# Token columns loaded at the start, earlier adding transfers, new strand shares: a six-stage hybrid network on one core

## The chip, the core and the metric

The kernel runs on one core of a Trainium2 chip. The metric is the device time of one execution in microseconds (us). TensorE appears as PE (its weight loads as PEld), VectorE as DVE, ScalarE as ACT, GpSimd as POOL, and SyncE as SP, which issues most of the transfers.

## What is computed

A two-layer network on 256 tokens of width 1024, in fp32: six stages, each followed by a residual sum and a layer norm. Four stages are gated feed-forward networks (FFN, width 2816), one is a hybrid of a gated delta rule and a state-space scan (SSD), one is a sparse attention (NSA).

```python
def swiglu(x, w_in, w_out):
    gate, up = jnp.split(x @ w_in, 2, axis=-1)
    return (jax.nn.silu(gate) * up) @ w_out
...
h = x
for layer in range(DEPTH):                 # DEPTH = 2
    h = layer_norm(ALPHA * h + 0.5 * swiglu(h, ffn_w_in[layer, 0], ffn_w_out[layer, 0]), ...)
    mix = hybrid_mixer(h, ...) if layer % 2 == 0 else nsa_mixer(h, positions, ...)
    h = layer_norm(ALPHA * h + mix, ...)
    h = layer_norm(ALPHA * h + 0.5 * swiglu(h, ffn_w_in[layer, 1], ffn_w_out[layer, 1]), ...)
```

The hybrid stage projects `h` to queries, keys, values and gates of the delta rule and of the scan, runs both over the tokens in chunks, and projects the two results back. The sparse attention adds three attentions (over compressed blocks, over chosen blocks, over a window) under gates, and projects back.

## The kernel before

**Stages.** FFN1 runs to about 172 us, the hybrid to 420, FFN2 to 583, FFN3 to 757, the NSA stage to 895, FFN4 to the end.

**Products.** Each large product is made of three with operands of a shorter format: high x high, low x high, high x low. SP loads a weight tile as it is (512 KB, `raw`), ACT writes its high part (`whi`, `split` at L660), DVE subtracts for the low part (`wlo`). The token columns have the same two parts (`x`, high and low, tokens as columns by blocks of 128 features) and, in an FFN, the whole values (`X`), from which `token_forms` (L734) makes sums for a product scheme with seven products in place of eight (`wide`, L751; parts `fhi`, `flo`).

**An FFN** (`ffn`, L1044) goes over its 2816 hidden columns in 22 blocks of 128 (`f`). Blocks 0 to 3 come first (in FFN1 by `first_steps`, L1011: two passes over the input, gate columns, then up columns, 48 products each, and in the other FFNs by row tiles). Blocks 4 and 5 come by column tiles. The rest come in `CHUNKS` = 4 chunks of four blocks by `wide`. Between the seven products of a chunk, `flush` does terms of the second matrix: for a block `f`, `out_mm` multiplies the block's activation (`gh`, `gl`) with row tile `f` of `w_out` into the four banks of `acc`. `weights_to` loads row tiles three ahead (`AHEAD`).

**Adding transfers.** For the row tiles of `ADDED` (8, 10, ..., 20: seven in an FFN, 28 in all) DVE does not make the low part: ACT writes minus the high part into `wlo`, and a transfer from POOL's queue adds the weight from memory to it (`rows`, L705). Tiles live in slots of one pool; `W` (raw, high and low parts) may use 28 of them, with 14 kept for it.

**The head.** `run` (L2103) starts with products on constants (`spin`), then loads the tokens row by row into `h0`, `h1` in four transfers of 256 KB (`load`), in between the first weight tiles (`first_weights`, L717, with `arrivals`), and transposes them on PE in sixteen 128 x 128 products (`transpose_half`); ACT and DVE copy the results out as `x` and `X`. `h0`, `h1` stay as the residual.

**The order.** A planner (`Plan`, L187) lists all operations first, prices each (L269), and then sets one order for each engine (`order`, L352), by when an operation's inputs are ready and a priority. All instructions come out at L561 (`emit`), so the trace has that line throughout. Inside the hybrid and the NSA stage the strands are interleaved by `weave` (L885) in proportion to shares: `W_HYB` for (delta, space, gate, space2, out_a), `W_NSA` for (attention, dense, compressed, out_g0). `dense` (L1875) are projections that wait for nothing but weights, `out_g0` (L2089) the first products of the output projection.

Of the kernel before, what the change touches and what calls it, by code (L numbers as in the profile page):

```python
# [50 lines left out]
CHUNKS, AHEAD, LAG = 4, 3, 7  # L51

TERMS = ((0, 1, 1, 1, 1, 1, 1), (0, 0, 1, 1, 1, 1, 0), (0, 0, 1, 1, 1, 1, 0), (0, 0, 1, 1, 1, 0, 0))

ADDED = range(8, 22, 2)

STRANDS = ("mp",)
W_HYB, W_NSA = (60.0, 140.0, 25.0, 40.0, 15.0), (70.0, 60.0, 40.0, 20.0)
# [3 lines left out]
RANK = 0  # L62

# [118 lines left out]
class Op:  # L182
    __slots__ = ("eng", "fn", "args", "kw", "idx", "prio", "cost", "table", "deps", "succ", "ndep", "ready", "start",
                 "end", "alloc", "dense", "alts", "tiles", "nbytes", "quad", "port", "banks")


class Plan:  # L187
# [11 lines left out]
    def __init__(self):  # L199
        self.ops = []  # L200
        self.tiles = []
        self.base = 0
        self.gate = None
        for e in ("tensor", "vector", "scalar", "gpsimd", "sync"):
            setattr(self, e, _Eng(self, e))
# [7 lines left out]
    def add(self, eng, fn, args, kw, alts=None):  # L213
# [3 lines left out]
        op.alts = alts  # L217
        op.deps, op.succ, op.alloc, op.nbytes = {}, [], None, 0
# [133 lines left out]
    def order(self, caps):  # L352
# [27 lines left out]
        port = 0.0  # L380
# [67 lines left out]
        while left:  # L448
            best = None
            for e in engs:  # L450
# [6 lines left out]
                for op in lst:  # L457
# [16 lines left out]
                    key = (st if st > f + 1e-9 else f, p)  # L474
                    if cand is None or key < cand[0]:
                        cand = (key, op, pen)
# [5 lines left out]
            (key, op, pen), e = best  # L482
            st = key[0] + pen
# [23 lines left out]
            if fn == "dma_start":  # L507

                at, need = st + 1300, op.nbytes * (2 if e == "gpsimd" else 1)
                while need > 0:  # L510
                    n = int(at / 500)
                    room = (155e3 if at < 8000.0 else 190e3) - moved.get(n, 0)
                    take = min(need, room, room * (n + 1 - at / 500), 95e3 if e == "gpsimd" else need)
# [3 lines left out]
                op.end = at + 600  # L517
# [67 lines left out]
class K:  # L585
    NT = 2
# [130 lines left out]
    def first_weights(self, w, n0, arrivals):  # L717

        out = []
        for n in range(4):  # L720
            src = w[n0 + n]
            raw = self.m4(1024, "raw", "W")
            hi, lo = (self.m4(1024, name, "W", F32R) for name in ("whi", "wlo"))
            step = 512 if arrivals and n < 2 else 1024
            for e in range(0, 1024, step):
                cs = slice(e, e + step)
                self.nc.sync.dma_start(raw[:, cs], src[:, cs])
                self.split(hi[:, cs], lo[:, cs], raw[:, cs])
                for f in (arrivals.pop(0) if arrivals else []):
                    f()  # L730
            out += [(hi[:, k * 512:k * 512 + 512], lo[:, k * 512:k * 512 + 512]) for k in range(2)]
        return out
# [207 lines left out]
    def layer_norm(self, b, acc, s, gb, x, last):  # L940
# [70 lines left out]
    def first_steps(self, x, w_in, gtiles, gts):  # L1011
# [4 lines left out]
        for c0, tag, arrivals in ((0, "acc", self.arrivals), (DFF, "ps", [])):  # L1016
# [15 lines left out]
        for b in range(2):  # L1032
# [6 lines left out]
            for f in range(4):  # L1039
                self.split(gts[f][0][:, b * P:(b + 1) * P], gts[f][1][:, b * P:(b + 1) * P], pt[:, f * P:(f + 1) * P])  # L1040
            with _Gate(self.plan, len(self.plan.ops) - 1):
                self.scale_h(b)

    def ffn(self, l, j, x, then, last=False):  # L1044
# [5 lines left out]
        NT = self.NT  # L1050
# [10 lines left out]
        def out_mm(b, f, g, wo, cols=range(2)):  # L1061
            for c in cols:
                cs = slice(c * 512, (c + 1) * 512)
                bs = slice(b * P, (b + 1) * P)
                n = count[b, c] = count.get((b, c), 0) + 1
                self.mm3(acc[b][c], (g[0][:, bs], g[1][:, bs]), (wo[0][:, cs], wo[1][:, cs]), n == 1,
                         n == NF - (ENDS if last and b == 1 and c == 1 else 0))
# [4 lines left out]
        else:  # L1072
# [4 lines left out]
            for b in range(2):  # L1077
                for s in range(NT):
                    ps = self.bank("ps")
# [12 lines left out]
        terms, late, wos = [], [], []  # L1092
# [1146 lines left out]
```

## Time and profile before

| | |
|---|---|
| three runs | 1090.65, 1086.72, 1089.8 us, median 1089.8 us |
| the profiled execution | 1087.19 us, its span (first to last instruction) 1085.5 us |
| mean granted TensorE clock | 0.995 of full speed |
| busy: PE, DVE, ACT | 1066.3, 1010.9, 725.9 us of the span |

The span leaves 1.7 us of the execution's time outside. Engines work side by side, so a busy time says only how long an engine had work; what its waits cost is to be seen at each place. The clock of a stretch is either its full level (2.4 GHz, 1.00) or its half (1.2 GHz, 0.50), or a mean of the two.

### The profile page before, as it was taken

The numbers are of one execution on the slowest core, as the hardware profiler recorded it, in microseconds if no ns is written. First come the engines' busy times: TensorE is split into PE (matmuls) and PEld (weight loads), VectorE is DVE, ScalarE is ACT, GpSimd is POOL, SyncE is SP. The second block draws the span as 40 slices with busy tenths as digits, with TensorE's granted clock in tenths as the row PEclk, the third lists the DMA queues.
The fourth block names the chain that finished last, engine by engine and source line by source line (L and its number), as shares of the span: only waits on it lengthen the run. The fifth ranks groups of instructions, "written<-read, shape, count | busy, mean of one in ns | idle before, by whom it ended". The sixth has DMA issues, their size and how long they took to land.

```text
span 1085.5 us, 16212 instructions
## 1 busy us (share of the span) xinstructions
PE 1066.3 (98%) x5946; PEld 893.3 (82%) x5946; DVE 1010.9 (93%) x1453; ACT 725.9 (67%) x1155; POOL 70.7 (7%) x116
## 2 busy tenths in 40 slices
PE   8999999998999999999999999999999999999997
PEld 6788888897999788888888888888887778888886
DVE  7999999799979999999999999999978889999995
ACT  7767866368737774667866667678465778666780
POOL 1000000001001310000000000000001000000000
PEclk9999999999999999999999999999999899999999
DMA  8658768535433575367777736679563336457881
GB/s 330 231 196 256 221 233 284 179 135 182 140 115 99 194 269 180 117 230 251 215 229 254 257 125 215 235 241 303 189 214 98 92 123 216 152 188 236 255 231 41
DMA packets 65034, 215.71 MB, mean 199 GB/s; under 512 B 8301, under 2 KB 12218, under 8 KB 64954
## 3 DMA queue, kind: packets, MB, share of 16 engines
q1 hardware_dynamic: 60922, 199.98, 52.8%
q0 software_dynamic: 4032, 14.68, 7.2%
q8 instruction: 47, 0.77, 0.3%
q14 instruction: 33, 0.27, 0.1%
HBM read 211.86 MB, written 1.07 MB: 196 GB/s over the span
## 4 chain that ended last, share of the span: by engine, by line
PE 84%; DVE 12%; ACT 1%; DMA 1%; issue 1%; POOL 0%; SPq 0%; DVEq 0%; ACTq 0%
PE ps L561 39%; PE acc L561 31%; PE mp L561 14%; DVE wlo L561 2%; DVE cv L561 2%; DVE arena L561 1%; DMA raw<-in_ffn_w_in_dram 1%; DVE o L561 1%; DVE sw L561 1%; DVE x L561 1%; DVE y L561 1%; DVE qs L561 1%; DVE AT L561 0%; POOL arena L561 0%; DVE Y L561 0%
## 5 line engine op out<-in xcount | busy, mean ns | idle before, releaser
L561 ACT ACTIVATE whi<-raw 128x1024 fp32r<-128x1024 f32 (+1 forms) x435 | 436.8, 1052 | 104.0 <-DVE raw L561 85.4
L561 DVE TENSOR_TENSOR wlo<-raw,whi 128x1024 fp32r<-128x1024 f32 (+2 forms) x419 | 491.4, 1205 | 7.1 <-ACT whi L561 6.1
L561 PE MATMUL ps<-whi,x 128*128 128x512 f32 (+1 forms) x864 | 234.8, 390 | 0.3 <-ACT cv L561 0.3
L561 PEld LDWEIGHTS ps<-whi,x 128*128 128x128 f32 x864 | 156.7, 188 | 30.6 <-issue 1.5
L561 DVE TENSOR_TENSOR raw<-raw,raw 128x1024 f32<-128x1024 f32 x128 | 152.8, 1216 | 0.0
L561 PE MATMUL ps<-wlo,x 128*128 128x512 f32 (+1 forms) x432 | 127.1, 385 | 0.0
L561 PE MATMUL ps<-x,whi 128*128 128x256 f32 (+2 forms) x560 | 114.3, 312 | 4.0 <-ACT cv L561 2.4
L561 PEld LDWEIGHTS ps<-x,whi 128*128 128x128 f32 (+1 forms) x560 | 90.4, 188 | 11.4 <-ACT cv L561 3.8
L561 PE MATMUL acc<-whi,gh 128*128 128x512 f32 x253 | 99.3, 393 | 0.0
L561 PE MATMUL acc<-wlo,gh 128*128 128x512 f32 x253 | 99.0, 391 | 0.0
L561 PE MATMUL acc<-whi,gl 128*128 128x512 f32 x253 | 97.9, 390 | 0.0
L561 PEld LDWEIGHTS ps<-wlo,x 128*128 128x128 f32 x432 | 79.6, 188 | 15.3 <-issue 0.4
L561 PE MATMUL ps<-x,wlo 128*128 128x256 f32 (+1 forms) x344 | 80.0, 284 | 0.5 <-DVE wlo L561 0.5
L561 PE MATMUL acc<-whi,x 128*128 128x512 f32 x224 | 73.7, 405 | 2.3 <-DVE x L561 0.8
L561 PE MATMUL acc<-whi,g 128*128 128x512 f32 x192 | 63.3, 392 | 0.0
L561 POOL DMA_DIRECT2D wlo<-in_ffn_w_out_dram x28 | 24.4, 872 | 569.2 <-ACT wlo L561 391.3
L561 PEld LDWEIGHTS ps<-x,wlo 128*128 128x128 f32 (+1 forms) x344 | 58.1, 189 | 2.1 <-DVE wlo L561 0.7
L561 PEld LDWEIGHTS acc<-whi,gl 128*128 128x128 f32 x253 | 47.5, 188 | 9.8
L561 PEld LDWEIGHTS acc<-whi,gh 128*128 128x128 f32 x253 | 47.5, 188 | 9.5
L561 PEld LDWEIGHTS acc<-wlo,gh 128*128 128x128 f32 x253 | 47.5, 188 | 9.5
L561 PEld LDWEIGHTS acc<-whi,x 128*128 128x128 f32 x224 | 41.8, 189 | 11.8 <-ACT whi L561 2.1
L561 PE MATMUL mp<-whi,fhi 128*128 128x512 f32 x128 | 49.9, 390 | 0.0
(284 smaller groups left out, 1735.2 us busy)
## 6 DMA issues: line engine op xcount, KB each, us to landing
raw<-in_ffn_w_in_dram SPq DMA_DIRECT2D x174, 512.0 KB, 5.5
raw<-in_ffn_w_out_dram SPq DMA_DIRECT2D x88, 512.0 KB, 3.7
wlo<-in_ffn_w_out_dram POOLq DMA_DIRECT2D x28, 512.0 KB, 8.5
raw<-in_hyb_w_col_dram SPq DMA_DIRECT2D x28, 512.0 KB, 4.5
raw<-in_hyb_w_tok_dram SPq DMA_DIRECT2D x16, 512.0 KB, 7.8
raw<-in_hyb_w_out_dram SPq DMA_DIRECT2D x16, 512.0 KB, 3.7
raw<-in_nsa_w_tok_dram SPq DMA_DIRECT2D x8, 512.0 KB, 6.6
raw<-in_nsa_w_one_dram SPq DMA_DIRECT2D x8, 512.0 KB, 5.8
```

The lines of the kernel that those rows point to most:

```text
L561: r = getattr(getattr(nc, eng), fn)(*[res(a) for a in args], **{k: res(a) for k, a in kw.items()})
```

## The change

1. **Tokens as columns.** The host hands the tokens over a second time, in the layout of the columns (`x_cols`). Four transfers of 256 KB bring them straight into `X`, each ahead of one of the first weight tiles (`first_loads`). ACT and DVE make `x` from `X` in four operations each of 512 columns. The transposes, the copies out of them, and the arrivals are gone. `h0`, `h1` are loaded later, in two transfers of 512 KB, for the residual alone. Of the first weight tiles only the first comes in halves. The spins are two of 512 columns.
2. **Adding transfers.** An added row tile is loaded two tiles earlier than the others (`EARLY`), and its low-part products are made one term later (`OWED`, `pay`). The planner prices the adding transfers anew (`ADD_RATE`, `ADD_LATE`, one after the other).
3. **Shares.** `W_HYB` and `W_NSA` have new numbers.
4. **A head start** of 135 ns, in the planner's choice, for the layer norm's operations on DVE and ACT (`HOT`).
5. **The rates' exponential** in the hybrid now waits in the plan for the sigmoid's exponential (`_Gate`).

`CHUNKS` becomes a tuple with 4 in all places, so the code for five chunks isn't used.

```diff
-ADDED = range(8, 22, 2)
+ADDED, EARLY, OWED = range(8, 22, 2), 2, 1
-W_HYB, W_NSA = (60.0, 140.0, 25.0, 40.0, 15.0), (70.0, 60.0, 40.0, 20.0)
+W_HYB, W_NSA = (51.0, 98.0, 22.0, 45.0, 20.0), (100.0, 67.0, 63.0, 21.0)
+HOT = 135.0
+ADD_RATE, ADD_LATE = 130e3, 4000.0
...
-                    key = (st if st > f + 1e-9 else f, p)
+                    at = st - HOT if op.hot and e in ("vector", "scalar") else st
+                    key = (at if at > f + 1e-9 else f, p)
...
+    def first_loads(self, x, w):
+        raws = []
+        for n in range(8):
+            if n < 4:
+                nc.sync.dma_start(x[1][n // 2][:, :, n % 2 * 2:n % 2 * 2 + 2, :],
+                                  self.i['x_cols'][n].rearrange("p (b k t) -> p b k t", b=2, k=2))
+            raw = self.m4(1024, "raw", "W")
+            for cs in [slice(0, 512), slice(512, 1024)] if n == 0 else [slice(0, 1024)]:
+                nc.sync.dma_start(raw[:, cs], w[n][:, cs])
+            raws.append(raw)
...
-            w = self.first_weights(w_in, 4 if c0 else 0, arrivals)
+            for n in range(4):
+                if c0 == 0:
+                    hi, lo = (x[0][n][:, :, e] for e in range(2))
+                    self.split(hi, lo, x[1][n // 2][...])
+                w += self.first_weights(raws.pop(0), [slice(0, 1024)] if c0 or n else [slice(0, 512), slice(512, 1024)])
...
+            with self.late():
+                nc.sync.dma_start(self.ah[b], self.i['x'][0, b * P:(b + 1) * P])
...
-            while len(wos) < min(n, NF):
-                wos.append(self.rows(w_out, len(wos), len(wos) in ADDED))
+            for f in range(NF):
+                if f not in wos and f < n + EARLY * (f in ADDED):
+                    wos[f] = self.rows(w_out, f, f in ADDED)
...
+                hi = (0,) if f in ADDED else (0, 1)
+                for b in both:
+                    out_mm(b, f, g, wos[f], parts=hi)
+                if f in ADDED:
+                    owed.append((done, both, f, g))
+                pay(done - OWED)
...
-        nc.scalar.activation(rate, rate, AF.Exp)
         self.sigmoid(beta, sm[:, :, 0:8])
+        with _Gate(self.plan, len(self.plan.ops) - 3):
+            nc.scalar.activation(rate, rate, AF.Exp)
...
-        spin(4, 2)
+        spin(4, 4)
...
-        load(0, 0)
-        with _Gate(self.plan, len(self.plan.ops) - 3):
-            spin(2, 2)
-        self.arrivals = [[], [lambda: load(1, 0)], [], [lambda: load(0, 1), lambda: load(1, 1)]]
```

**What moves at the head, on PE.** `ones` are the spins, `mp<-ident,h` the transposes, `acc<-whi,x` the first pass. Before:

```order
L561 MATMUL acc_124<-ones_109 128x512
L561 MATMUL acc_124<-ones_109 128x256
L561 MATMUL mp_143<-ident_126,h_3_111 128x128 x4
L561 MATMUL acc_161<-whi_151,x_157 128x512 x4
L561 MATMUL acc_124<-ones_109 128x256
L561 MATMUL acc_161<-wlo_167,x_157 128x512
L561 MATMUL acc_124<-ones_109 128x256
L561 MATMUL acc_161<-wlo_167,x_157 128x512
L561 MATMUL mp_178<-ident_126,h_5_116 128x128 x4
L561 MATMUL mp_183<-ident_126,h_3_111 128x128 x4
```

Now:

```order
L573 MATMUL acc_128<-ones_109 128x512 x2
L573 MATMUL acc_168<-whi_163,x_157 128x512 x2
L573 MATMUL acc_172<-whi_163,x_157 128x512 x2
L573 MATMUL acc_168<-whi_163,x_157 128x512 x2
L573 MATMUL acc_172<-whi_163,x_157 128x512 x2
L573 MATMUL acc_168<-wlo_166,x_157 128x512 x2
L573 MATMUL acc_172<-wlo_166,x_157 128x512 x2
L573 MATMUL acc_168<-whi_187,x_177 128x512 x4
```

Only the two spins stand ahead of the first pass, and nothing stands between its products. On ACT the scaling of the residual (`h`) now stands ahead of the high part of the first column tile (`whi_318`, blocks 4 and 5); it stood behind all four of these and two more. Now on ACT:

```order
L573 ACTIVATE whi_264<-raw_140 128x1024
L573 ACTIVATE sg_275<-acc_172 128x512
L573 ACTIVATE fhi_284<-X_3_111 128x1024
L573 ACTIVATE fhi_296<-X_8_123 128x1024
L573 ACTIVATE h_43_262<-h_43_262 128x512 x2
L573 ACTIVATE h_45_266<-h_45_266 128x512 x2
L573 ACTIVATE whi_318<-raw_268 128x1024
```

`whi_318` thus waits for the transfers of `h_43` and `h_45`, which stand ahead of its own on SP's queue too.

**What moves with an added tile, on PE.** `gh`, `gl` are the activation's parts of block 8 of FFN1, the first added one. Before, low-part and high-part products stand together:

```order
L561 MATMUL acc_605<-whi_912,gh_850 128x512
L561 MATMUL acc_605<-wlo_903,gh_850 128x512
L561 MATMUL acc_605<-whi_912,gl_859 128x512
L561 MATMUL acc_613<-whi_912,gh_850 128x512
L561 MATMUL acc_613<-wlo_903,gh_850 128x512
```

Now the high-part products come first, and some forty rows of the list later the four of the low part:

```order
L573 MATMUL acc_528<-whi_709,gh_803 128x512
L573 MATMUL acc_528<-whi_709,gl_812 128x512
L573 MATMUL acc_537<-whi_709,gh_803 128x512
L573 MATMUL acc_537<-whi_709,gl_812 128x512
...
L573 MATMUL acc_528<-wlo_701,gh_803 128x512
L573 MATMUL acc_537<-wlo_701,gh_803 128x512
L573 MATMUL acc_543<-wlo_701,gh_803 128x512
L573 MATMUL acc_555<-wlo_701,gh_803 128x512
```

No product is added; four of one term are made a term later.

**What moves at the end of the attention, on PE.** `ps<-whi,x` and `ps<-wlo,x` are the dense strand, `ident` and `kd`, `qs` the attention, `acc<-whi,x` the output projection. Before, the last dense product and what follows:

```order
L561 MATMUL ps_8350<-whi_8196,x_7693 128x512
L561 MATMUL ps_8506<-fixed_3924 128x512
L561 MATMUL mp_8509<-ident_126,P_8352 128x128 x2
L561 MATMUL mp_8509<-ident_126,P_8395 128x128 x2
...
L561 MATMUL mp_8573<-ident_126,arena_8273 128x128
L561 MATMUL mp_8577<-arena_7865,qT_1476_7874 128x32 x4
L561 MATMUL mp_8594<-ident_126,P_8430 128x128 x2
...
L561 MATMUL acc_8626<-whi_8215,x_8472 128x512
```

Now:

```order
L573 MATMUL ps_8304<-whi_8161,x_7658 128x512
L573 MATMUL mp_8509<-ident_132,P_8426 128x128
L573 MATMUL mp_8513<-ident_132,P_8426 128x128
...
L573 MATMUL ps_8521<-fixed_4059 128x512
L573 MATMUL acc_8543<-whi_8183,x_8356 128x512
L573 MATMUL acc_8543<-wlo_8191,x_8356 128x512
L573 MATMUL acc_8543<-whi_8183,x_8356 128x512
L573 MATMUL mp_8555<-ident_132,P_8426 128x128 x2
```

Between the last dense product and the first of the output projection stood 31 rows of the list; now there are 12, and from there on projection and attention alternate.

## Rows read from the trace of the kernel before

**Rows 1.** The page's first part: busy time of each engine, its share of the span and its instructions, of the whole execution.

```profile
PE 1066.3 (98%) x5946; PEld 893.3 (82%) x5946; DVE 1010.9 (93%) x1453; ACT 725.9 (67%) x1155; POOL 70.7 (7%) x116
```

**Rows 2.** Busy time by stretch (start:end in us, the stretch's length, then for PE, PEld, DVE, ACT and POOL the busy time with the instructions in brackets, the mean granted clock of TensorE, the DMA engines' mean busy share, GB/s).

```profile
5.00:10.00 5.00, 3.65 (x17) 2.74 (x18) 2.59 (x6) 1.27 (x4) 0.00 (x0) 1.00 0.95 306
10.00:15.00 5.00, 4.24 (x21) 3.11 (x20) 3.83 (x9) 5.00 (x13) 0.00 (x0) 1.00 1.03 420
15.00:30.00 15.00, 15.00 (x68) 12.43 (x67) 15.00 (x16) 13.11 (x16) 0.00 (x0) 1.00 0.84 300
45.00:172.00 127.00, 127.00 (x580) 105.31 (x580) 126.07 (x128) 93.92 (x112) 6.19 (x7) 1.00 0.72 227
255.00:270.00 15.00, 12.00 (x84) 10.50 (x84) 14.93 (x38) 14.32 (x27) 0.00 (x0) 1.00 0.53 150
375.00:380.00 5.00, 4.34 (x22) 3.06 (x21) 5.00 (x12) 4.38 (x10) 1.20 (x1) 1.00 0.78 287
500.00:510.00 10.00, 10.00 (x46) 8.28 (x45) 10.00 (x9) 9.97 (x12) 0.87 (x1) 1.00 1.04 313
845.00:850.00 5.00, 3.11 (x19) 2.50 (x18) 4.94 (x14) 4.85 (x19) 1.21 (x5) 0.86 0.50 162
850.00:855.00 5.00, 4.53 (x20) 4.23 (x21) 4.75 (x10) 4.47 (x16) 0.00 (x0) 0.50 0.01 2
855.00:860.00 5.00, 5.00 (x27) 2.70 (x27) 2.34 (x8) 2.15 (x10) 0.00 (x0) 0.95 0.00 0
```

**Rows 3.** The timeline of PE over the opening (start, duration of the run of like instructions, operation, out<-in, shape, count, idle time before it and its releaser).

```profile
3.79 1.06 PE L561 MATMUL mp<-ident,h 128*128 128x128 f32 x4
...
5.46 1.06 PE L561 MATMUL acc<-whi,x 128*128 128x512 f32 x2 [0.61 <-DVE x L561]
...
7.35 0.73 PE L561 MATMUL acc<-whi,x 128*128 128x512 f32 x2 [0.83 <-ACT whi L561]
...
13.24 2.01 PE L561 MATMUL acc<-whi,x 128*128 128x512 f32 x8
...
31.41 1.07 PE L561 MATMUL ps<-wlo,x 128*128 128x512 f32 x4
...
33.59 2.08 PE L561 MATMUL ps<-x,whi 128*128 128x512 f32 x8 [1.11 <-DVE sg L561]
```

**Rows 4.** The timeline of ACT over the opening, with the same columns.

```profile
4.41 0.63 ACT L561 ACTIVATE whi<-raw 128x512 fp32r<-128x512 f32 x1 [2.10 <-DMA raw<-in_ffn_w_in_dram]
...
6.67 0.63 ACT L561 ACTIVATE whi<-raw 128x512 fp32r<-128x512 f32 x1 [1.63 <-DMA raw<-in_ffn_w_in_dram]
...
31.55 1.28 ACT L561 ACT_TABLE_LOAD   x1
...
35.28 2.26 ACT L561 ACTIVATE whi<-raw 128x1024 fp32r<-128x1024 f32 x2 [2.21 <-DMA raw<-in_ffn_w_in_dram]
...
38.96 2.26 ACT L561 ACTIVATE h<-h 128x512 f32<-128x512 f32 x4
```

**Rows 5.** What DVE waited for from 0 to 180 us (total us, times, longest).

```profile
DVE wlo L561 <- ACT whi L561: 3.2, 5, 1.2
DVE x L561 <- ACT x L561: 3.0, 1, 3.0
```

**Rows 6.** The timeline of DVE over the opening: what one low part, one half of a low part and one operation on the tokens takes.

```profile
4.88 0.76 DVE L561 CAST x<-mp 128x256 fp32r<-128x256 f32 x2 [3.08 <-PE mp L561]
...
5.56 0.75 DVE L561 TENSOR_TENSOR x<-mp,x 128x256 fp32r<-128x256 f32 x2
...
6.22 0.68 DVE L561 TENSOR_TENSOR wlo<-raw,whi 128x512 fp32r<-128x512 f32 x1
...
13.79 0.68 DVE L561 TENSOR_TENSOR X<-X,X 128x512 f32<-128x512 f32 x1
...
27.62 1.22 DVE L561 TENSOR_TENSOR wlo<-raw,whi 128x1024 fp32r<-128x1024 f32 x1
```

**Rows 7.** The timeline near the end of the first FFN: ACT's operation for a tile whose low part an adding transfer makes, two low parts on DVE, and the products on PE that use the second of these.

```profile
150.92 1.05 ACT L561 ACTIVATE wlo<-raw 128x1024 fp32r<-128x1024 f32 x1
...
150.97 2.35 DVE L561 TENSOR_TENSOR wlo<-raw,whi 128x1024 fp32r<-128x1024 f32 x2
...
153.89 0.62 PE L561 MATMUL ps<-wlo,fhi 128*128 128x512 f32 x2
```

**Rows 8.** The page's sixth part: the adding transfers (count, KB each, median us from issue to landing).

```profile
wlo<-in_ffn_w_out_dram POOLq DMA_DIRECT2D x28, 512.0 KB, 8.5
```

**Rows 9.** The timeline of PE in the last stretch of the sparse attention.

```profile
842.85 0.40 PE L561 MATMUL ps<-whi,x 128*128 128x512 f32 x1
...
845.36 0.71 PE L561 MATMUL ps<-kd,qs 128*128 128x256 f32 x4
...
847.79 0.30 PE L561 MATMUL mp<-ident,arena 128*128 128x128 f32 x1 [0.79 <-DVE arena L561]
...
848.92 1.92 PE L561 MATMUL mp<-arena,qT 128*128 128x32 f32 x8 [0.83 <-ACT arena L561]
...
852.19 1.05 PE L561 MATMUL ps<-kd,qs 128*128 128x256 f32 x4
...
855.39 0.43 PE L561 MATMUL acc<-whi,x 128*128 128x512 f32 x1
```

**Rows 10.** The timeline of the last microseconds: the layer norm's last operations on DVE, after PE's last product.

```profile
1080.81 1.54 DVE L561 SCALAR_TENSOR_TENSOR h<-h,lnve,lnb 128x512 f32<-128x512 f32 x3
```

More of the change, by code (lines that the diff above doesn't have):

```diff
@@ L183 @@
     __slots__ = ("eng", "fn", "args", "kw", "idx", "prio", "cost", "table", "deps", "succ", "ndep", "ready", "start",
-                 "end", "alloc", "dense", "alts", "tiles", "nbytes", "quad", "port", "banks")
+                 "end", "alloc", "dense", "alts", "tiles", "nbytes", "quad", "port", "banks", "hot")
 class Plan:
@@ L512, in order @@
                     room = (155e3 if at < 8000.0 else 190e3) - moved.get(n, 0)
-                    take = min(need, room, room * (n + 1 - at / 500), 95e3 if e == "gpsimd" else need)
+                    take = min(need, room, room * (n + 1 - at / 500), ADD_RATE if e == "gpsimd" else need)
                     moved[n] = moved.get(n, 0) + take
@@ L715, in rows, with first_weights @@
         return hi, lo
[L717 to L721, printed above, removed]
-            raw = self.m4(1024, "raw", "W")
[L723 to L732, printed above, removed]
+    def first_loads(self, x, w):
+        nc = self.nc
+        raws = []
[3 more added lines that the diff above has]
+                                  self.i['x_cols'][n].rearrange("p (b k t) -> p b k t", b=2, k=2))
+            raw = self.m4(1024, "raw", "W")
+            for cs in [slice(0, 512), slice(512, 1024)] if n == 0 else [slice(0, 1024)]:
+                nc.sync.dma_start(raw[:, cs], w[n][:, cs])
+            raws.append(raw)
+        return raws
+    def first_weights(self, raw, parts):
+        hi, lo = (self.m4(1024, name, "W", F32R) for name in ("whi", "wlo"))
+        for cs in parts:
+            self.split(hi[:, cs], lo[:, cs], raw[:, cs])
+        return [(hi[:, k * 512:k * 512 + 512], lo[:, k * 512:k * 512 + 512]) for k in range(2)]
     def token_forms(self, x):
@@ L1049, in ffn @@
         NF = DFF // P
-        NT = self.NT
+        CH = CHUNKS[2 * l + j]
+        NT = 2 if CH < 5 else 1
         pairs = {}
@@ L1059, in ffn, with out_mm @@
         count = {}
-        def out_mm(b, f, g, wo, cols=range(2)):
+        def out_mm(b, f, g, wo, cols=range(2), parts=(0, 1)):
             for c in cols:
@@ L1064, in out_mm @@
                 bs = slice(b * P, (b + 1) * P)
-                n = count[b, c] = count.get((b, c), 0) + 1
-                self.mm3(acc[b][c], (g[0][:, bs], g[1][:, bs]), (wo[0][:, cs], wo[1][:, cs]), n == 1,
-                         n == NF - (ENDS if last and b == 1 and c == 1 else 0))
+                for part in parts:
+                    n = count[b, c] = count.get((b, c), 0) + 1
+                    end = n == 2 * (NF - (ENDS if last and b == 1 and c == 1 else 0))
+                    nc.tensor.matmul(acc[b][c], g[0][:, bs], wo[part][:, cs], start=n == 1, stop=end)
+                    if part == 0:
+                        nc.tensor.matmul(acc[b][c], g[1][:, bs], wo[0][:, cs], start=False, stop=False)
         gts = {}
@@ L1078, in ffn @@
                 for s in range(NT):
[L1079 removed]
+                    ps = self.bank("ps" if NT > 1 else "acc")
                     self.proj_tok(x, b, steps[s], ps)
@@ L2194, in laid_out @@
             else:
-                t = [rows(np.concatenate([g[:, c:c + 256], u[:, c:c + 256]], 1), 2) for c in (0, 256)]
+                t = [rows(np.concatenate([g[:, c:c + 256], u[:, c:c + 256]], 1), 2) for c in ((0, 256) if CH < 5 else (0,))]
             for c in range(512, steps * 256, 256):
```

72 lines of the change are left out of this document (46 added, 26 removed).

## The prediction

> **What bounds the kernel now.** The page's first part comes first: PE is busy for 1066.3 of 1085.5 us [rows 1]. Only its 19.2 idle us, and stretches in which it runs slowly, can be won by another order. So the next view is busy time by stretch [rows 2]. From 45 to 172 us PE is never idle, and in 500 to 510 neither: in the FFN stages there is nothing to win on PE. It is idle for 1.35 us in 5 to 10, 0.76 in 10 to 15, 3.00 in 255 to 270, 0.66 in 375 to 380, and 1.89 + 0.47 in 845 to 855. The same rows show the clock at half from 850 to 855, and partly in the stretches beside it. The timelines then say who is waited for: in the opening transfers, ACT and DVE [rows 3, 4], in the attention small operations of DVE and ACT [rows 9]. The second thing to see is DVE: 126.07 of 127 us busy in FFN1 [rows 2]. Near its end a pair of low parts starts at 150.97, takes 2.35 and so is done at 153.32; PE uses the second at 153.89, 0.57 us later [rows 7]. In FFN1 DVE is thus as much a bound as PE.
>
> **The opening.** On PE, the sixteen transposes go, and of the spins only two long ones are left, at the very start. The first product still waits for the first half tile, whose high part ACT starts at 4.41 [rows 4], so it comes at about 5.4, as now (5.46, [rows 3]). The second half's high part starts at 6.67 in both. Behind it come 256 KB of tokens and the 512 KB of the second tile, 0.79 MB, at 306 to 420 GB/s [rows 2]: 1.9 to 2.6 us, so 8.6 to 9.3. With 1.05 us for its high part the second group of products starts at about 10.0 (estimate). From there 84 products remain in the two passes. Before, 84 ran from 13.24 to the end of the group at 31.41, which is 0.9 long: 19.1 us [rows 3]. So the second pass ends at 29.1 instead of 32.3: **-3.2** on PE. The wait of 1.11 us behind it, for DVE's gate, stays: the transposes of the gate now stand one product behind the pass and need the same operation.
>
> DVE must follow, or PE gives this back before 172 us. Its work up to the last activation of FFN1 loses 2 casts and 8 subtractions at 0.38, and 2 half low parts at 0.68; it gains 4 operations of 512 columns at 0.68 (priced as the like one at 13.79) and one low part at 1.22 [rows 6]: 1.2 us less. It can start at 4.0 instead of 4.88, since the first tokens had landed by 3.79, when PE transposed them [rows 3]. Its waits were 3.0 + 3.2 us, and 0.3 more [rows 5]. New ones come (estimates from the times above): about 1.6 for the second half tile, 1.0 for the second tile, and 2 ahead of the first column tile, since ACT scales the residual first (2.26, now at 38.96, [rows 4]) and 1 MiB more is loaded ahead of it; about 1.5 more come later in the stage, as now. Some 6 us against 6.5. DVE thus ends FFN1 between 1 and 2.5 us earlier. I take **-1.5** for the opening. The bounds are 0, all given back, and -3.2 - 0.5, with the small slack of DVE used up as well.
>
> The two later transfers of `h` are 2 x 512 KB, or 2.5 us at 420 GB/s. They push the loads behind them; ACT waited 2.21 us for one of these at 35.28, while PE was in a run of products from 33.59 on for which it had its tiles [rows 3, 4]. That run hides them; without that cover they cost up to 2.5 us, which the bound of 0 takes in.
>
> The clock in the opening: two products of 512 columns took 1.06 us at 5.46 and two took 0.62 us at 153.89 [rows 3, 7], so the first ones ran at the half level, although the row of the stretch says 1.00; by 13.24 eight take 2.01, the full level. I charge no change. The Trainium skill (TensorE: Matmul & The Clock Gate, "What's actually happening" and "PE-mode transpose") says that the half level is the default which only activity lifts, and that transposes do not count as activity in the same way; by this the removed spins would matter and the removed transposes would not. By that rule the second group of products could start at half level and the sum would be -3.5 in place of -5.0; the trace agrees as far as the fall to half at 850 us, behind PE's gaps, goes [rows 2].
>
> **Adding transfers, low part later.** No product is added or removed. They move in stages in which PE has no gap [rows 2], and ACT's step (1.05) and the transfer (8.5 to landing) stay [rows 7, 8]. A gain has nowhere to come from: **0**; the cost, if a slot runs out, is a rival below. **Head start of the layer norms:** the norms stand at borders of stages, where no row shows PE idle, except the last one, which has DVE to itself (its last three operations, 1.54 us, at 1080.81, [rows 10]): **0**. **The rates' exponential:** a table load of 1.28 us on ACT leaves FFN1 [rows 4]; ACT has spare time there (93.92 of 127): **0**, between -0.5 and 0.
>
> **Hybrid.** Up to about 280 us the order of PE is the same as before, so the 3.00 us of 255 to 270 stay; there DVE and ACT are busy for 14.93 and 14.32 of 15 us [rows 2]. Behind that only small waits such as the 0.66 of 375 to 380 are open to new shares, and new tight places can arise: **0**, between -2 and +2.
>
> **Attention.** From the last dense product at 842.85 to the first of the output projection at 855.39 PE had only the attention's own chain [rows 9]. It was idle 2.36 us in 845 to 855, and the clock fell. Time at half level: (1 - 0.86) x 2 x 5 + 5 + (1 - 0.95) x 2 x 5 = 6.9 us, in which PE was busy about 6; at full level half of that would go, 3.0 (four products of 256 columns took 1.05 at 852.19, and 0.71 at 845.36, [rows 9], so it is rather less). In sum up to -5.4. Now 12 rows of the list stand where 31 stood, and the output projection alternates with the attention. Against the full sum speaks that ACT and DVE are busy for 9.32 and 9.69 of these 10 us: the chain itself needs this long, and PE must be fed from elsewhere. I take **-3.5**, nearer to the full sum since the fill is there in the order; the bounds are 0 and -5.4.
>
> **Sum.** -1.5 - 3.5 = -5.0. Against the profiled execution (1087.19, of which 1.7 lie outside its span) that is 1082.2. This execution lies 2.6 us below the median of the three runs, 1089.8; against the median the forecast is **1084.8 us**.
>
> **Rivals.**
> 1. *Everything is kept* (0.24). DVE finds enough slack, the clock in the attention never falls: -3.2 - 5.4 = -8.6, so **1081.2**. For it: DVE's idle 3.0 us behind its first low parts goes. Against it: DVE at 126.07 of 127.
> 2. *The attention is bound by ACT and DVE* (0.16). The gaps only move, and the clock falls elsewhere: -1.5 alone, **1088.3**. For it: 9.32 and 9.69 of 10 us.
> 3. *The clock stays low in the opening* (0.08). PE waited 0.61 and 0.83 us ahead of its first products [rows 3] and will again, and no spins stand between them any more. If products run at half level as long as at 850 us, some 6 us, 3 are lost: -1.5 + 1.5 (DVE takes only 1.5 of PE's 3.2, so of 3 lost on PE all of it goes) - 3.5 = -3.5, **1086.3**.
> 4. *Slower: early tiles hold slots* (0.12). An added tile occupies three of 28 slots two tiles longer. If this makes the raw loads of other tiles late, each of the seven puts one load of 512 KB (1.25 us at 420 GB/s) into DVE's path. It decides once the delay is over DVE's lead, which is 0.57 us in FFN1 [rows 7]. In two such stages: 2 x 7 x 1.25 = 17.5, so +12.5, **1102**. Against it: ACT is free for 33 of 127 us there, and transfers have 28% to spare [rows 2].
>
> The forecast itself has 0.40. That the change does nothing is excluded by the order, which differs in all the places above.
>
> **Numbers.** 0.5% is 5.4 us, about what a measurement of this kernel can tell from no change; faster means below 1084.4. Of the forecast's 0.40 a little under half lies there (0.18), and all of rival 1: 0.42. Rival 4 is slower: 0.12. The rest, 0.46, is no change. The range leaves out rival 4 and reaches from rival 1 with its unknowns (hybrid -2, and a little more: 1077.5) to rival 2 with the hybrid's +2 and the opening's bound of 0, 1091.5.
>
> **What would show it.** Right: the first pass starts its second group near 10 us and the second pass ends near 29; DVE's waits in 20 to 30 us are new, and PE has gaps that wait for DVE's low parts before 172 us, or products at the end of FFN1 only 1 to 2.5 us earlier; 255 to 270 as it was; the clock at 1.00 in the stretch of the attention's end and the output projection, with PE's idle time there under 1 us. Wrong: the FFN stages with idle PE behind `raw` loads (rival 4), a clock below 1.00 anywhere else, or new waits in the hybrid of more than 2 us.

## The result, and the profile after

The changed kernel takes 1082.93 us (median of 6 runs, 1081.67 to 1084.38), the kernel before, beside it, 1089.55 (6 runs, 1086.22 to 1090.65): a ratio of 0.9948 [0.993, 0.9966]. In a later run, as a control among the experiments, it was 1083.93 against 1087.93, 0.9963 [0.9951, 0.9975]. The forecast was 1084.8; the time lies in its range, a little below its middle. The profiled execution took 1084.36, its span 1082.7.

First the page's first part, after. It answers to [rows 1]: PE has 2.0 us less to do, and it is idle for 18.4 us where it was idle for 19.2.

```profile
PE 1064.3 (98%) x5926; PEld 889.6 (82%) x5926; DVE 1016.7 (94%) x1456; ACT 722.2 (67%) x1142; POOL 72.4 (7%) x112
```

Busy time by stretch, after, answers to [rows 2] (start:end, length, then PE, PEld, DVE, ACT, POOL, granted clock, DMA share, GB/s):

```profile
0.00:172.00 172.00, 168.01 (x749) 135.91 (x749) 159.70 (x171) 123.13 (x155) 9.67 (x27) 1.00 0.77 257
5.00:10.00 5.00, 3.89 (x13) 2.85 (x14) 2.42 (x5) 2.70 (x5) 0.00 (x0) 1.00 0.95 329
10.00:15.00 5.00, 5.00 (x22) 4.12 (x23) 4.38 (x6) 3.60 (x5) 0.00 (x0) 1.00 1.04 415
15.00:30.00 15.00, 14.58 (x65) 11.77 (x64) 13.20 (x14) 12.55 (x16) 0.00 (x0) 1.00 0.94 358
45.00:172.00 127.00, 125.77 (x564) 102.87 (x562) 125.14 (x123) 92.70 (x108) 6.20 (x7) 1.00 0.72 231
172.00:200.00 28.00, 25.97 (x117) 20.88 (x118) 25.34 (x41) 12.90 (x23) 2.00 (x2) 0.94 0.57 212
255.00:270.00 15.00, 12.10 (x85) 10.70 (x84) 14.92 (x38) 14.65 (x29) 0.00 (x0) 1.00 0.48 149
845.00:850.00 5.00, 4.43 (x27) 3.19 (x26) 5.00 (x11) 5.00 (x19) 0.48 (x1) 1.00 0.67 229
850.00:855.00 5.00, 5.00 (x29) 2.78 (x28) 5.00 (x10) 5.00 (x14) 1.33 (x4) 1.00 0.25 87
855.00:860.00 5.00, 5.00 (x43) 3.79 (x43) 4.64 (x12) 2.67 (x11) 0.00 (x0) 1.00 0.24 64
```

The same view of the kernel before, for two stretches that were not shown:

```profile
0.00:172.00 172.00, 167.08 (x761) 136.87 (x762) 161.50 (x180) 127.60 (x167) 9.66 (x27) 1.00 0.75 248
172.00:200.00 28.00, 28.00 (x132) 22.95 (x131) 26.78 (x46) 12.65 (x20) 2.00 (x2) 1.00 0.70 253
```

Three things stand out. In the attention's end (845 to 855) PE's idle time fell from 2.36 us to 0.57 and the clock stays at 1.00. From 255 to 270 nothing changed. And at the end of FFN1 PE, which had no gap there before, now has 1.23 us in 45 to 172 and 2.03 in 172 to 200: **3.26 us**, as much as the opening won.

The timeline of PE over the opening, after, against [rows 3]:

```profile
5.26 2.84 PE L573 MATMUL acc<-whi,x 128*128 128x512 f32 x8 [0.42 <-ACT whi L573]
...
9.88 2.11 PE L573 MATMUL acc<-whi,x 128*128 128x512 f32 x8 [0.85 <-ACT whi L573]
...
28.15 1.07 PE L573 MATMUL ps<-wlo,x 128*128 128x512 f32 x4
29.64 0.47 PE L573 MATMUL ps<-x,whi 128*128 128x512 f32 x1 [0.42 <-DVE sg L573]
```

The second group starts at 9.88 and the second pass ends at 29.2, 3.3 us earlier. Here is what DVE waited for from 0 to 180 us, after, against [rows 5]:

```profile
DVE wlo L573 <- ACT whi L573: 5.8, 7, 1.8
DVE x L573 <- ACT x L573: 4.2, 2, 2.8
...
DVE gl L573 <- ACT gh L573: 0.7, 1, 0.7
...
DVE sg L573 <- ACT sg L573: 0.5, 2, 0.3
```

How far DVE is can be read off at one landmark, the first operation on the activation of FFN1's last chunk. In the timeline of DVE, before:

```profile
159.68 0.68 DVE L561 TENSOR_TENSOR vg<-mp,vg 128x512 f32<-128x512 f32 x1
```

and after:

```profile
161.40 0.68 DVE L573 TENSOR_TENSOR vg<-mp,vg 128x512 f32<-128x512 f32 x1
```

PE came out of the opening 3.3 us earlier, but DVE reaches this point 1.72 us **later**. The busy times from 0 to the landmark, before and after (columns as above), say why:

```profile
0.00:159.68 159.68, 154.76 (x703) 126.58 (x704) 149.26 (x167) 116.30 (x154) 8.26 (x26) 1.00 0.73 242
0.00:161.40 161.40, 157.97 (x705) 127.91 (x706) 149.10 (x159) 114.26 (x146) 9.12 (x27) 1.00 0.75 251
```

The low parts ahead of the landmark are as many in both (75 whole ones and four halves before, 76 and two after). DVE has 0.16 us less to do up to there (149.10 against 149.26), and it is idle for 12.30 us in place of 10.42. So PE runs into DVE and what hangs on it. PE's timeline at that place, after:

```profile
157.06 0.50 PE L573 MATMUL ps<-whi,fhi 128*128 128x512 f32 x1 [0.55 <-ACT su L573]
...
171.98 0.63 PE L573 MATMUL mp<-ident,vg 128*128 128x128 f32 x4 [0.55 <-DVE vg L573]
174.25 1.22 PE L573 MATMUL acc<-whi,gh 128*128 128x512 f32 x2 [1.64 <-ACT gh L573]
```

The last row also shows the clock: two products take 1.22 us, where two take 0.62 at the full level; 170 to 180 us has a mean of 0.83. In the control's profiled execution nearly the same gaps stand there, the two products take 0.73 and the clock of 170 to 180 is 1.00:

```profile
172.10 0.63 PE L573 MATMUL mp<-ident,vg 128*128 128x128 f32 x4 [0.55 <-DVE vg L573]
174.30 0.73 PE L573 MATMUL acc<-whi,gh 128*128 128x512 f32 x2 [1.57 <-ACT gh L573]
```

So the fall is not part of every execution; the gaps are.

The next table lines up PE's products of two traces by the work that is still to do behind each of them (every kind of product at its median time in the kernel before; where the order of two kernels differs, as at 840, this is good to some tenths), and gives how many us a kernel is behind the kernel before (negative: ahead) at that point. It is worked out from all rows of PE; the profiled execution of before is the zero of all columns.

| at (us of before) | 30 | 100 | 150 | 190 | 420 | 760 | 840 | 860 | 1060 |
|---|---|---|---|---|---|---|---|---|---|
| changed kernel | -3.3 | -4.7 | -4.1 | 1.5 | 0.8 | 0.9 | 1.5 | -2.9 | -3.0 |
| changed kernel, control | -3.1 | -4.5 | -4.0 | 0.0 | 0.0 | 0.0 | 0.6 | -3.9 | -3.9 |
| opening alone | -2.2 | -3.4 | -1.4 | 6.3 | 6.6 | 7.7 | 7.7 | 7.5 | 7.4 |
| NSA shares alone | -1.1 | -1.1 | -1.1 | -1.4 | -1.3 | -1.2 | -1.0 | -5.4 | -5.1 |
| change with old opening | 0.6 | -0.2 | -0.1 | -0.1 | -0.7 | 1.1 | 1.6 | -2.9 | -3.0 |
| change, adding transfers as before | -3.1 | -4.6 | -2.6 | -0.6 | 0.0 | 5.8 | 6.1 | 1.7 | 1.5 |
| change, no head start | -2.6 | -4.1 | -3.5 | 2.1 | 1.6 | 4.4 | 4.6 | 0.2 | 0.5 |
| change, four low parts less | -2.0 | -3.4 | -3.2 | -3.1 | -3.3 | -3.2 | -2.7 | -7.1 | -7.2 |
| the same with zeros in the slots | -3.3 | -4.8 | -4.7 | -3.4 | -3.7 | -3.7 | -3.1 | -7.5 | -7.7 |

In the control the whole lead of the opening is gone at 190 us, nothing changes up to 760, and the NSA stage gives 3.9 us. From 760 to 1060 it is 3.9 us in the changed kernel's first trace and in that of the NSA shares alone too. (The row of the NSA shares alone is 1.1 ahead from the first 10 us on, where its code is that of before; that is how far executions differ.)

### The profile page after: what moved, and what is told of

It is laid out like the page before. It is cut to its first block, busy times and chain, and to the rows that moved or that the text cites. A ratio compares the mean times of both kernels' runs of the same rounds, so it can differ in the third digit from the quotient of the medians.

```text
span 1082.7 us, 16152 instructions
## 1 busy us (share of the span) xinstructions
PE 1064.3 (98%) x5926; PEld 889.6 (82%) x5926; DVE 1016.7 (94%) x1456; ACT 722.2 (67%) x1142; POOL 72.4 (7%) x112
## 5 line engine op out<-in xcount | busy, mean ns | idle before, releaser
L573 ACT ACTIVATE whi<-raw 128x1024 fp32r<-128x1024 f32 (+2 forms) x431 | 431.0, 1050 | 81.1 <-DVE raw L573 68.4
L573 PE MATMUL ps<-wlo,x 128*128 128x512 f32 (+1 forms) x432 | 130.1, 388 | 0.0
L573 PE MATMUL acc<-wlo,gh 128*128 128x512 f32 x253 | 85.5, 390 | 0.0
L573 PE MATMUL ps<-whi,fhi 128*128 128x512 f32 x128 | 50.2, 392 | 0.7 <-ACT su L573 0.5
```

The lines of the kernel that those rows point to most:

```text
L573: r = getattr(getattr(nc, eng), fn)(*[res(a) for a in args], **{k: res(a) for k, a in kw.items()})
```

## The experiments

Each was timed in five rounds beside the kernel before on the same chip; ratios are to that. The changed kernel was run again on one of these chips only, so elsewhere it is the ratios that are set side by side. In the diffs, `...` stands for what is left out.

**Opening alone.** The kernel before with the new opening; everything else as before.

```diff
-ADDED, EARLY, OWED = range(8, 22, 2), 2, 1
-W_HYB, W_NSA = (51.0, 98.0, 22.0, 45.0, 20.0), (100.0, 67.0, 63.0, 21.0)
-HOT = 135.0
-ADD_RATE, ADD_LATE = 130e3, 4000.0
+ADDED, EARLY, OWED = range(8, 22, 2), 0, 0
+W_HYB, W_NSA = (60.0, 140.0, 25.0, 40.0, 15.0), (70.0, 60.0, 40.0, 20.0)
+HOT = 0.0
+ADD_RATE, ADD_LATE = 95e3, 0.0
...
+        nc.scalar.activation(rate, rate, AF.Exp)
...
```

> The new opening alone: tokens as columns, with the adding transfers, both sets of shares, the head start and the rates' exponential as before. My theory (DVE and the loads set the end of FFN1, so what PE wins in the opening is given back by 190 us): second pass ends near 29 us, but the whole run is only 0.5 to 1.5 us faster than before, 1088 to 1089. Rival (the opening's gain on PE of 3.2 us stays): 1086.3 or less. In the trace the theory expects new waits of PE between 150 and 190 us of 2 us or more; the rival none.

Measured: 1093.97 against 1087.02, 1.0061 [1.0049, 1.0073]: slower by 7 us; both theories missed the time. PE's waits from 45 to 200 us in its trace:

```profile
PE acc L573 <- DMA wlo<-in_ffn_w_out_dram: 4.2, 3, 1.6
PE mp L573 <- DVE h L573: 2.1, 1, 2.1
PE ps L573 <- DVE x L573: 1.4, 1, 1.4
```

The opening is ahead by 2.2 us at 30, and then PE meets the adding transfers, which land too late for an earlier PE, and the layer norm. Its landmark on DVE is at 162.18, 2.5 us later than before, although one low part fewer stands ahead of it. By itself the opening is no gain but a loss.

**Changed kernel with the old NSA shares.**

```diff
-W_HYB, W_NSA = (51.0, 98.0, 22.0, 45.0, 20.0), (100.0, 67.0, 63.0, 21.0)
+W_HYB, W_NSA = (51.0, 98.0, 22.0, 45.0, 20.0), (70.0, 60.0, 40.0, 20.0)
```

> The changed kernel with the old shares in the sparse attention. My theory (the attention's end gives the larger part of the gain, 3.5 to 5): PE idle and the clock at half near 845 to 855 us return, and the run takes 1086.4 to 1088 us. Rival (the gain comes from elsewhere, the attention is bound by ACT and DVE): 1083 to 1084, no more than 1 us above the changed kernel.

Measured: 1087.35 against 1087.02, 1.0006 [0.9997, 1.0016]. All of the gain is gone. The stretch of the attention's end is what it was in the kernel before, 2.36 us idle and a clock of 0.77:

```profile
845.00:860.00 15.00, 12.64 (x62) 9.30 (x60) 13.01 (x33) 13.73 (x54) 1.19 (x4) 0.77 0.22 70
```

**Kernel before with the new NSA shares alone.**

```diff
-W_HYB, W_NSA = (60.0, 140.0, 25.0, 40.0, 15.0), (70.0, 60.0, 40.0, 20.0)
+W_HYB, W_NSA = (60.0, 140.0, 25.0, 40.0, 15.0), (100.0, 67.0, 63.0, 21.0)
```

> The kernel before with nothing changed but the shares of the sparse attention. My theory: 3.5 to 5 us faster than before, 1084.5 to 1086, the clock at 1.00 between 840 and 865 us. Rival: within 1 us of before, 1088.5 to 1090.5.

Measured: 1083.52 against 1087.02, 0.9967 [0.9954, 0.998]. The four numbers alone give what the whole change gives. The same stretch, with the clock at its full level:

```profile
845.00:850.00 5.00, 4.55 (x25) 3.03 (x27) 5.00 (x9) 5.00 (x10) 1.81 (x4) 1.00 0.62 210
850.00:855.00 5.00, 5.00 (x30) 2.60 (x28) 4.96 (x11) 3.80 (x15) 0.00 (x0) 1.00 0.01 2
855.00:860.00 5.00, 5.00 (x52) 4.59 (x47) 3.73 (x11) 3.88 (x18) 0.33 (x1) 1.00 0.69 181
```

**Where the opening's lead goes, first try.** In the changed kernel's trace ACT waits 1.59 us for a weight tile of the hybrid at 171.22, ahead of the activation's `su` and `gh`. Here the high parts of these tiles, all but the first, wait in the plan for FFN1's last `gh`.

```diff
+                self.done = len(self.plan.ops) - 2
...
-        ws = [self.row_tiles([w_in[c0 + 4 * c + n] for n in range(4)], 2) for c in range(2)]
...
+                raw = self.arrive(w_in[c0 + 4 * c + n])
+                self.plan.gate = self.done if 4 * c + n >= 1 else None
+                hi, lo = self.halved(raw)
...
```

> The changed kernel, in which the high parts of the hybrid's first weight tiles (all but the first) wait in the plan for FFN1's last activation, so that no ACT operation that waits for a late load stands ahead of it. My theory of the lost opening (PE's wait of 1.64 us for gh at 174 us, and the clock's fall behind it, come from ACT's queue: an operation waits 1.59 us there for a load): no fall of the clock near 174 us, and 1 to 3 us faster than the changed kernel, 1080 to 1082. Rival (the loads are late anyway, and PE then waits for the hybrid's first weights): the wait moves behind 185 us, and the time stays within 0.7 us of the changed kernel, 1082.2 to 1083.6.

Measured: 1084.1 against 1087.02, 0.9969 [0.9957, 0.9981], as the changed kernel: my theory's time missed. The wait for `gh` shrinks from 1.6 us to 0.2, but PE's idle time from 45 to 200 us is 2.97 instead of 3.26: a wait of 1.06 for the layer norm's `h`, at 185.78, takes its place. ACT behind a late transfer was the last link there, not the cause.

**Changed kernel as it is**, the control for the next three.

> The changed kernel itself, on the chip of the next three, so that they have it beside them: 0.993 to 0.997 of before.

Measured: 1083.93 against 1087.93, 0.9963 [0.9951, 0.9975].

**Changed kernel, adding transfers as before.**

```diff
-ADDED, EARLY, OWED = range(8, 22, 2), 2, 1
-ADD_RATE, ADD_LATE = 130e3, 4000.0
+ADDED, EARLY, OWED = range(8, 22, 2), 0, 0
+ADD_RATE, ADD_LATE = 95e3, 0.0
...
```

> The changed kernel with the adding transfers as before (not loaded earlier, low part in its own term, old prices in the planner). Theory A (the early opening runs into the adding transfers: with the new opening alone PE waited 4.2 us for three of them): PE waits 3 us or more for wlo from memory, and the run is 3 to 6 us slower than the changed kernel. Theory B (what the opening alone lost, it lost in FFN1's layer norm, where PE waited 2.05 and 1.40 us for DVE's h and x; the head start mends it): within 1 us of the changed kernel, and no such wait above 1 us.

Measured: 1085.8, 0.9985 [0.9976, 0.9993], 1.9 us over the control, between the two theories. PE waits for two adding transfers (1.5 us in all) in FFN1, half of what theory A asked for, and without a loss by 190 us. In the profiled execution the price comes in FFN2, most of it at its end, where the clock falls too (0.91 in 580 to 600 us). But this execution lies 3.1 us over its kernel's median, so the 5.8 of the table at 760 is more than the usual price, and where the usual 1.9 us arise is not shown. PE's waits from 420 to 800 us are for DVE, not for a transfer:

```profile
PE mp L573 <- DVE vg L573: 3.6, 2, 2.5
```

**Changed kernel without the head start** of the layer norms.

```diff
-HOT = 135.0
+HOT = 0.0
```

> The changed kernel without the head start of the layer norms (0 ns). Theory A: within 1 us of the changed kernel. Theory B: 2 to 4 us slower, with waits of PE for DVE's h or x behind a layer norm.

Measured: 1087.53, 0.9995 [0.9987, 1.0004], 3.6 us over the control. In its trace PE waits for the layer norm itself:

```profile
187.80 1.29 PE L573 MATMUL mp<-ident,h 128*128 128x128 f32 x8 [1.70 <-DVE h L573]
```

From 172 to 200 us PE is busy for 24.26 us, in the control for 25.93. In the table 2.1 us are lost by 190 against 0.0 in the control; behind that, 1.6 at 420 become 4.4 at 760. Theory B is borne out.

**Changed kernel with the old opening**: `first_loads`, the spins, the transposes and the loads of `h` as in the kernel before, everything else of the change kept.

```diff
-        raws = self.first_loads(x, w_in)
...
+            w = self.first_weights(w_in, 4 if c0 else 0, arrivals)
...
-        spin(4, 4)
+        spin(4, 2)
...
```

> The opening of the kernel before with all other parts of the change. My theory (what the opening wins on PE is given back by 190 us, and the attention gives the whole difference): within 1 us of the changed kernel, with the second pass ending near 32 us and no waits of PE from 150 to 190 us. Rival (the opening's 3.2 us are a part of the gain): 2 to 3.5 us slower than the changed kernel.

Measured: 1084.57, 0.9971 [0.996, 0.9983], 0.6 us over the control; their intervals overlap by about two thirds. PE has no idle time from 45 to 200 us here, and DVE reaches the landmark at 158.72, 2.7 us before the changed kernel. (Some 1.1 of these 2.7 are one low part that stands behind the landmark here; 1.2 are less idle time.) What the new opening saves is given back by 190 us.

**Less work for DVE at FFN1's end.** Four row tiles have no low part of their own (the kernel leaves that part of the sum out), so DVE has 4 x 1.14 us less to do.

```diff
+        if bare:
...
+            nc.scalar.activation(hi, raw, AF.Copy)
+            return hi, hi
...
-                    wos[f] = self.rows(w_out, f, f in ADDED)
+                    wos[f] = self.rows(w_out, f, f in ADDED, l + j == 0 and f in (11, 13, 15, 17))
```

> The changed kernel in which FFN1's row tiles 11, 13, 15 and 17 of the second matrix get no low part of their own (their high part is used twice): 4 x 1.14 us of DVE's work and 4 slots less, the same products on PE. It leaves that part of the sum out. Theory D (DVE sets the end of FFN1, and gives the opening back): PE's lead of 4 us over the old opening is kept to 190 us, its waits between 150 and 190 us go, 2 to 4 us faster than the changed kernel (1083.9 beside 1087.9 of before). Theory L (the loads at FFN1's end set it): within 1 us of the changed kernel.

Measured: 1079.82 against 1087.84, 0.9928 [0.9916, 0.9941], some 3.8 us below the changed kernel, as theory D had it. The gaps of FFN1's end are gone:

```profile
45.00:172.00 127.00, 127.00 (x575) 104.59 (x574) 125.14 (x125) 96.58 (x114) 6.21 (x7) 1.00 0.75 243
172.00:200.00 28.00, 28.00 (x133) 23.03 (x132) 26.92 (x43) 10.81 (x20) 2.00 (x2) 1.00 0.57 186
```

DVE's landmark is at 157.97, 3.4 us earlier: up to there DVE is busy for 144.57 us in place of 149.10, which is 4 x 1.13 less, and idle for 1.10 us more. PE had no gap from 45 to 200 us with the old opening, so these are gains on the gaps that came with the new one.

**Less to load at FFN1's end.** The first layer norm's scale and shift are not loaded but set by GpSimd, 1 MiB less at about 156 us.

```diff
+            if l + j == 0:
+                self.nc.gpsimd.memset(t, 1.0)
+                continue
```

> The changed kernel in which the scale and shift of the first layer norm are set on POOL to 1 and are not loaded (2 x 512 KB less to transfer at 156 us, 2.5 us at 420 GB/s; it leaves the real ones out). Theory L: the hybrid's first tiles land 2.5 us earlier, ACT's wait for one of them at 171 us goes, and the run is 1.5 to 3 us faster than the changed kernel. Theory D: within 1 us of it.

Measured: 1084.4, 0.9976 [0.9964, 0.9987]: no gain. ACT's wait at 171 us is gone, as theory L had it, but PE's idle time from 45 to 200 us is still 3.07, most of it now at DVE's products, and the landmark is at 161.22. The 1 MiB of this stretch is not what binds.

**DVE's work moved to transfers.** Three more tiles of FFN1 get their low part by an adding transfer.

```diff
+        ad = sorted([*ADDED, 6, 11, 15]) if l + j == 0 else ADDED
...
-                if f not in wos and f < n + EARLY * (f in ADDED):
-                    wos[f] = self.rows(w_out, f, f in ADDED)
+                if f not in wos and f < n + EARLY * (f in ad):
+                    wos[f] = self.rows(w_out, f, f in ad)
```

> The changed kernel with three more adding transfers in FFN1 (tiles 6, 11 and 15, ten in place of seven): 3 x 1.14 us of DVE's work go to the transfers, nothing is left out. Theory D: 1.5 to 3 us faster than the changed kernel. Theory L: the same or slower by up to 3 us, with waits of PE for wlo from memory or of ACT for raw tiles.

Measured: 1084.78, 0.9978 [0.9967, 0.9988]: no gain: theory D's time missed, theory L's came, but without the waits that it named. DVE's busy time from 45 to 172 falls to 122.94, but its landmark stays at 161.45: up to there it is busy for 145.94 us (149.10 in the changed kernel) and idle for 15.51 (12.30). The work it lost is replaced by waits; what DVE waited for from 0 to 180 us:

```profile
DVE wlo L573 <- ACT whi L573: 8.0, 9, 1.9
DVE x L573 <- ACT x L573: 2.9, 1, 2.9
DVE vg L573 <- ACT vg L573: 1.9, 2, 1.0
```

Each adding transfer costs ACT another operation of 1.05 us [rows 7], and DVE waits more for ACT. That the one makes the other is argued, not shown.

**Work or slots?** The run with less work for DVE also freed four slots, into which loads could come earlier. Here each of the four tiles keeps its slot.

```diff
+            lo = self.m4(1024, "wlo", "W", F32R)
...
+            with _Gate(self.plan, len(self.plan.ops) - 1):
+                nc.gpsimd.memset(lo.bitcast(F32), 0.0)
...
```

> The changed kernel, in which the row tiles 11, 13, 15 and 17 of the first feed-forward's first half have no low part of their own on VectorE, as in the run with less VectorE work there (that part of the sum is left out), but each still takes a low-part slot, which GpSimd fills with zeros: VectorE's work in 45 to 172 us is 4 x 1.14 = 4.6 us less, the number of slots in use is as in the changed kernel. Theory D (the lead of the new opening is lost because VectorE's own work ends too late at the first feed-forward's end): 3 to 4 us faster than the changed kernel, a ratio of about 0.993 to the kernel before, TensorE at 10.00 in the windows of 10 us from 150 to 190. Theory S (it is lost because low parts hold the slots that the next raw tiles' loads wait for; four free slots let them start earlier): within 1 us of the changed kernel, 0.996 to 0.998, and the waits at 156 and 171 us stay.

Measured: 1079.32 against 1087.7, 0.9924 [0.9912, 0.9936]. Theory D's time, with one gap of 1.05 us left (160 to 170 us), which theory D had not allowed. DVE's landmark is at 156.41. The slots are not the cause. One path is not separated: without the subtraction the raw tile's slot is free when ACT has read it, not when DVE has. Either way it is DVE's part of the work that holds PE up; which of the two paths does it is not shown.

## Why the prediction was right, and where not

| step | forecast (us) | measured (us) |
|---|---|---|
| second group starts | 10.0 | 9.88 |
| second pass ends earlier by | 3.2 | 3.3 |
| DVE's work up to FFN1's end | -1.2 | -0.16 up to the landmark |
| DVE ahead at FFN1's end | 1 to 2.5 | -1.72 |
| opening, kept | -1.5 (0 to -3.7) | -0.6, not told from 0 |
| adding transfers, new for old | 0 | -1.9 with the rest of the change |
| head start | 0 | -3.6 with the rest of the change |
| hybrid | 0 | 0.0 from 190 to 420 in the control |
| attention | -3.5 (0 to -5.4) | -3.5 by itself; -3.9 from 760 to 1060 |
| sum | -5.0 | -4.0 and -5.7 by the two ratios |

**Attention: right.** Place, cause and nearly the size came as forecast. Idle time 2.36 to 0.57, clock 1.00 instead of 0.86, 0.50 and 0.95. PE's timeline there, after, answers to [rows 9]:

```profile
849.00 0.50 PE L573 MATMUL ps<-fixed 128*128 128x512 f32 x1 [0.31 <-ACT P L573]
...
850.48 0.40 PE L573 MATMUL acc<-whi,x 128*128 128x512 f32 x1
...
851.71 2.79 PE L573 MATMUL acc<-PT,vtok 128*64 128x512 f32 x12
```

The first product of the output projection comes at 850.48 (855.39 before), and one wait of 0.31 us is all that is named of the chain's. Without the new shares the gain is gone, and by themselves they give it. Rival 2, that ACT and DVE need these 10 us anyway, is refuted: they are now busy for all of them (10.00 and 10.00), and PE still lost only 0.57, with other products to do meanwhile.

**Opening: the mechanism right, one step wrong.** PE's times came to 0.12 us, and PE gives its lead back before and just behind 172 us at DVE's products and what hangs on them. The first new waits of DVE were about as long as forecast: 1.41 us ahead of its second operation on the tokens (in the control 1.29 ahead of the second half tile, where 1.6 was put), 1.17 ahead of the second tile (1.0), 1.80 ahead of the first column tile (2). Wrong was "DVE thus ends FFN1 between 1 and 2.5 us earlier", in all three of its terms:

- *Work.* It was to be 1.2 us less; up to the landmark it is 0.16 less. The ten small operations that went had taken 3.3 us and not 10 x 0.38, since each starts before the last one ends (two take 0.76, but the next pair starts 0.68 behind, [rows 6]), and others take about 0.5 us more now.
- *Start.* It was to be 4.0; it is 4.59. DVE's first operation takes ACT's high part of the tokens, and ACT starts on that at 3.93, for 0.63 us; the forecast had left this step out.
- *Waits.* They were to be "some 6 us against 6.5". The rows show 5.8 + 0.7 + 0.5 (for the gate) and, of the 4.2, 1.4 (the other 2.8 stand ahead of its first operation): 8.4, or 7.7 without the 0.7, which stands behind the landmark. DVE waits for ACT's high part ahead of seven low parts (five before), three of them at 91, 123 and 156 us, 1.75 us together.

DVE's idle time from 0 to 172 us rose from 10.50 to 12.30 instead of falling. So -1.5 should have been the bound that stood beside it, 0. Rival 1, everything kept, falls with this step: with DVE relieved the lead is kept (3.1 us at 190 in place of 0), so what it lacked was DVE. PE's lead was even larger than forecast, 4.7 us at 100, since the wait of 1.11 us for the gate behind the second pass did not stay: it is 0.42.

**The zeros: wrong as prices of their own.** "They move in stages in which PE has no gap" was true of the kernel before. But the opening makes PE meet DVE, ACT and the transfers 3 us earlier, and in this state the stages have gaps: the opening alone costs 7 us, and with it in place the adding transfers' change gives 1.9 and the head start 3.6. In the kernel with the old opening all these parts together change little up to 420 us (-0.7), and in FFN2 and FFN3 they lose 1.8. They don't make a gain; they pay for what the opening would cost. The new hybrid shares and the rates' exponential had no run of their own, so their part is not known.

**The sum** came out near in part by luck: the opening was taken about 1 us too high (-1.5 against -0.6), the attention up to 0.4 too low, and the zeros of the adding transfers and the head start fit the sum only because what these two save (1.9 and 3.6) is what the opening alone would lose.

**Rivals 3 and 4.** Rival 3 was seen in part, at almost no cost. The first eight products, at 5.26, took 2.84 us where eight take 2.01 at the full level, and in the control 4.00, all of them at the half level; the second group took 2.11 and 2.00. But the control's second group started at 10.17, only 0.29 later than 9.88, for the slow products filled the wait that stood ahead of it (0.85 us):

```profile
5.40 4.00 PE L573 MATMUL acc<-whi,x 128*128 128x512 f32 x8 [0.55 <-ACT whi L573]
9.23 1.10 PE L573 MATMUL acc<-wlo,x 128*128 128x512 f32 x4
10.17 2.00 PE L573 MATMUL acc<-whi,x 128*128 128x512 f32 x8
```

The Trainium skill (TensorE: Matmul & The Clock Gate, "What's actually happening") has the half level as the default that activity lifts; the trace agrees for the first eight products, and by the second group the level was up, without the spins that stood there before. Rival 4, a loss of 17.5 us, did not come. One of the signs that it named is there in a small way: ACT stood 1.59 us at a raw tile of the hybrid ahead of `gh`, for which PE waited 1.64 us; taking that wait away gave nothing. The adding transfers land after 7.3 us ([rows 8] had 8.5); but in the control it is 7.7, and with the adding transfers as before 7.8, so this is no sign of the earlier loads:

```profile
wlo<-in_ffn_w_out_dram POOLq DMA_DIRECT2D x28, 512.0 KB, 7.3
```

Another sign that the prediction gave for being wrong was seen too, a clock below 1.00 elsewhere: 0.83 from 170 to 180 us, in one of two profiled executions of the changed kernel. It belongs to the opening's step that failed.

**No version** of the whole computation beat the changed one: the four numbers alone and the change with the old opening are level with it. The two runs with fewer low parts show that about 4 us more lie in DVE's work in FFN1.

**Open** is which of DVE's waits makes how much of the 1.72 (none was taken away by itself), whether DVE's own time or the raw tiles that it holds delays PE, and why nearly equal gaps were followed by a fall of the clock in one profiled execution and not in the other.

## What to carry to other kernels

Where two engines are both nearly full, a start that frees one of them is worth what the other can follow: find a landmark on the second engine near the stage's end and ask whether *it* comes earlier, with its waits counted tile by tile. An edit that costs nothing beside a full engine can decide the result once another edit has moved that engine, so edits made together have to be priced in the state that they make. A chain of small operations need not be shortened to be hidden: give the idle engine independent products there, and it keeps its clock as well.

## What the hardware showed that was not expected

The clock after short gaps is not the same from run to run: behind gaps of 0.55 and 1.64 us PE's clock fell (0.83 in 170 to 180 us), behind 0.55 and 1.57 at the same place it did not (1.00). With less to load it fell there again (0.83), behind gaps of 0.56, 1.02 and 0.44. The fall cost about 1.5 us, an estimate from two executions (1.5 against 0.0 at 190 us in the table). The clock's rise at the start differs as well: the same first eight products took 2.84 us in one execution of the changed kernel and 4.00 in another. At the attention's end eight transposes in a row at 844.27 took 1.03 us, and more of them stand among products up to 850; the clock stayed at 1.00 throughout.
